# Second block of a two-block Trainium2 kernel: its input transposed without the norm's factor, which is applied behind the products

## The chip, the cores and the metric

The kernel is one program on 1 core of one Trainium2 chip. The metric is the device time of one execution in microseconds (us). Three runs of the kernel before took 1331.56, 1333.13 and 1335.11 us; the median is 1333.13 us.

Engine names: PE is TensorE's matmul, PEld its weight load, DVE VectorE, ACT ScalarE, POOL GpSimd, SP SyncE (here it issues transfers only).

## What is computed

Two blocks follow each other over 512 tokens of width 1024. The first (normalised projection, stick-breaking attention beside an RWKV-7 group, output projection, a mixture of 32 experts) ends in `rmsnorm(h, final_norm_g)`. That is the input x of the second, cut here to what the change touches:

```
h = rms_norm(x, norm_gain)                     # x * rsqrt(mean(x*x) + 1e-6) * gain
proj = h @ w_in
qa, ka, va, qb, kb, vb, ga, gb, mg = split(proj)
qa = head_rms_norm(qa, q_norm_a) * scale       # per head of 64
ka = head_rms_norm(ka, k_norm_a)
ya = banded_attention(qa, ka, va, ...) * silu(ga)
qb, kb = head_rms_norm(qb) * scale, head_rms_norm(kb)
yb = (softmax-weighted sum of three dilated groups of qb, kb, vb) * silu(gb)
gates = sigmoid(mg + b_merge)
merged = gates[0] * (ya @ w_branch_a) + gates[1] * (yb @ w_branch_b)
x = x + merged @ w_out
```

Both norms before `w_in` multiply each token by one number, so x reaches `w_in` as h * r * (final_norm_g * norm_gain), with one r per token.

## The kernel before

Tokens are four tiles of 128 (index i, NT = 4) and the width is eight blocks of 128 (index k, KD = 8). Every float32 product is made of three matmuls on rounded halves: `split` (L197) writes a high part by ACT (L206, or L203 without a scale) and a low part by DVE (L207, or L204), and `mm3` (L210) multiplies high by high (L212), high by low and low by high (L213, L214). The Tile framework's scheduler sets the order of each engine's instructions; a few calls pin it.

**End of block one.** `combine` (L1313) adds the experts' result to the residual tile `hres`: for each token tile and half of the width a group of matmuls `cb` (L1320) into PSUM, then one DVE add (L1324). In its last call it runs `last(i)` (L1345) behind each token tile. That makes both norms' sums, by an ACT square with a sum (L1354) and by a DVE multiply-and-sum (L1359; for tile 0 by POOL and ACT, L1356 and L1357), the factor r by a power on POOL (L1363), and a diagonal matrix `dg3` of it (L1364). `ahead` (L1328) has loaded and split the first section of the second block's weights.

**Start of the second block** (`phase3`). `turn(k, i0, n)` (L1478) makes block k of the transposed input: a matmul of a tile of `hres` with `dg3` (L1483) transposes it and multiplies by r at once. Two tiles share a call; `split` with the scale gg then gives `ah` and `al` (L206 and L207 on 128x256), 16 times.

**The sections.** `w_in` is 33 sections of 256 columns, each a 1 MB load (`load`, L1467) on SP's queue. A token-major section (`tok`, L1508) makes 96 matmuls `tm` in two halves of the weights; a feature-major one (`fm`, L1535) 48 matmuls `fm` over 512 tokens, in two. The first, at 0 and 256, are q of attention A, 512 is its k and v. `normed` (L1547) gives each token tile to a sink: squares on ACT (L1542), a copy to `raw` (L1543), a DVE reduction to `qss` (L1544), then `rsqrt` (DVE L282, POOL power L287, four numbers a token). `turned` (L1551) scales `raw` on DVE to `qsc` (L1555), transposes it on PE (`qT`, L1559) and copies it by ACT (L1561). `after_k` sends v through DRAM by POOL's queue (L1649, L1650). Gates (`gated`, L1864: sigmoid on ACT, two DVE multiplies, L1871 to L1873, and a split) and merge gates (`mg_sink`, L1908) are feature-major. The normalised x is written to DRAM from `hres` (DVE L1856, SP L1858).

## Time and profile before

| | |
|---|---|
| median of 3 runs | 1333.13 us |
| the profiled execution | 1333.91 us |
| its span, first to last instruction | 1331.9 us |
| PE busy | 1231.4 us, 92% of the span |
| DVE, ACT, POOL busy | 701.0, 483.3 and 231.6 us |
| mean granted TensorE clock | 0.958 of full |

The span is what the rows cover; the other 2.0 us of the execution lie around it. Times of rows count from the start of the span. A row of a timeline gives start, duration, engine, line, operation, and in brackets the idle time before it with what ended it. A busy PE is not PE at full speed: the granted clock (PEclk) has two levels, 1.00 (2.4 GHz) and 0.50 (1.2 GHz).

### The profile page before, as it was taken

What the parts mean: (1) busy time and instruction counts of PE and PEld (TensorE: products, weight loads), DVE (VectorE), ACT (ScalarE), POOL (GpSimd) and SP (SyncE); (2) the same over time, 40 slices, a digit from 0 to 9 for tenths busy, and PEclk for the clock granted to TensorE, in tenths of its full rate; (3) what the DMA queues carried; (4) which work ended last, traced back from release to release, by engine and by line L of the source; (5) the groups of instructions that cost most, each with busy time, mean ns of one, the idle gap of its engine ahead of it and who ended that gap; (6) DMA issues with size and microseconds to landing.
All of it is one profiled execution on the core that took longest, in us unless ns stands there. A gap on an engine that the chain in (4) does not pass through costs nothing.

```text
span 1331.9 us, 22066 instructions
## 1 busy us (share of the span) xinstructions
PE 1231.4 (92%) x8889; PEld 965.8 (73%) x8889; DVE 701.0 (53%) x1603; ACT 483.3 (36%) x999; POOL 231.6 (17%) x323
## 2 busy tenths in 40 slices
...
GB/s 310 77 39 57 57 41 32 33 64 52 140 102 390 257 389 422 422 422 421 424 184 69 121 78 64 88 62 99 70 92 65 82 81 64 145 93 79 80 140 67
DMA packets 45050, 198.87 MB, mean 149 GB/s; under 512 B 11639, under 2 KB 14105, under 8 KB 27792
## 3 DMA queue, kind: packets, MB, share of 16 engines
...
q14 instruction: 34, 0.28, 0.1%
...
## 4 chain that ended last, share of the span: by engine, by line
PE 50%; issue 9%; DVE 3%; ACT 3%; POOL 1%; DMA 1%; ACTq 0%; DVEq 0%; POOLq 0%
PE tm L212 7%; PE tm L213 7%; PE tm L214 7%; PE gu L1260 6%; PE fm L214 4%; PE fm L212 4%; PE fm L213 4%; PE pd L1283 3%; PE az L1601 2%; PE pbT L1818 1%; PE qT L1559 1%; ACT Pb L1612 1%; PE oa L1700 1%; PE paT L1686 1%; DMA fd<-znt 1%
## 5 line engine op out<-in xcount | busy, mean ns | idle before, releaser
L212 PE MATMUL tm<-wh,ah 128*128 128x256 f32 x800 | 231.6, 290 | 5.3 <-ACT vb L1726 5.3
L214 PE MATMUL tm<-wh,al 128*128 128x256 f32 x800 | 227.3, 284 | 0.0
L213 PE MATMUL tm<-wl,ah 128*128 128x256 f32 x800 | 227.0, 284 | 0.3 <-DVE wl L204 0.3
L204 DVE TENSOR_TENSOR wl<-w,wh 128x1024 fp32r<-128x1024 f32 (+1 forms) x124 | 144.9, 1169 | 149.1 <-ACT wh L203 148.7
L203 ACT ACTIVATE wh<-w 128x1024 fp32r<-128x1024 f32 (+1 forms) x124 | 124.1, 1002 | 260.3 <-PE tm L213 96.5
L212 PEld LDWEIGHTS tm<-wh,ah 128*128 128x128 f32 x800 | 152.2, 190 | 12.2 <-ACT vb L1726 5.5
L213 PEld LDWEIGHTS tm<-wl,ah 128*128 128x128 f32 x800 | 152.5, 191 | 0.8 <-DVE wl L204 0.6
L214 PEld LDWEIGHTS tm<-wh,al 128*128 128x128 f32 x800 | 151.8, 190 | 1.4 <-issue 1.3
L287 POOL TENSOR_TENSOR qss<-qss,nhalf 128x4 f32<-128x4 f32 x60 | 63.6, 1074 | 200.6 <-DVE qss L282 200.3
L212 PE MATMUL u<-xh,wh 128*128 128x512 f32 x176 | 75.7, 430 | 5.1 <-ACT xh L371 4.2
L212 PE MATMUL fm<-ah,wh 128*128 128x512 f32 x192 | 76.0, 396 | 0.0
L214 PE MATMUL fm<-ah,wl 128*128 128x512 f32 x192 | 75.9, 395 | 0.1
L213 PE MATMUL fm<-al,wh 128*128 128x512 f32 x192 | 75.9, 395 | 0.0
L214 PE MATMUL u<-xh,wl 128*128 128x512 f32 x176 | 73.7, 419 | 2.0 <-DVE wl L204 2.0
L213 PE MATMUL u<-xl,wh 128*128 128x512 f32 x176 | 74.3, 422 | 1.3 <-DVE xl L372 1.3
L1260 PE MATMUL gu<-eg,xgT 128*64 128x256 f32 x512 | 66.9, 396 | 2.3 <-DMA eg<-in_exp_w_gate_dram 1.9
L1283 PE MATMUL pd<-ed,hTs 128*64 128x512 f32 x256 | 64.8, 600 | 2.6 <-ACT hTs L1273 2.1
L1260 PE MATMUL gu<-eu,xgT 128*64 128x256 f32 x512 | 63.3, 380 | 0.0
L1263 ACT ACTIVATE hm<-gu 128x256 f32<-128x256 f32 x16 | 6.1, 384 | 146.1 <-PE gu L1260 101.6
L1264 DVE TENSOR_TENSOR hm<-hm,gu 128x256 f32<-128x256 f32 x16 | 6.7, 420 | 98.1 <-ACT hm L1263 98.1
L1260 PEld LDWEIGHTS gu<-eg,xgT 128*64 128x64 f32 x512 | 38.5, 142 | 26.3 <-issue 8.3
L1260 PEld LDWEIGHTS gu<-eu,xgT 128*64 128x64 f32 x512 | 39.5, 137 | 19.8 <-issue 2.3
...
## 6 DMA issues: line engine op xcount, KB each, us to landing
w<-in_w_dram SPq DMA_DIRECT2D x33, 1024.0 KB, 4.8
eg<-in_exp_w_gate_dram SPq DMA_DIRECT2D x32, 1024.0 KB, 19.7
eu<-in_exp_w_up_dram SPq DMA_DIRECT2D x32, 1024.0 KB, 19.4
ed<-in_exp_w_down_dram SPq DMA_DIRECT2D x32, 1024.0 KB, 19.7
...
yd<-hres POOLq DMA_DIRECT2D x1, 4096.0 KB, 15.9
...
yt<-yd SPq DMA_DIRECT2D x4, 1024.0 KB, 19.8
```

The costliest lines, as they stand in the source:

```text
L203: i = nc.scalar.activation(hi, src, AF.Copy)
L204: j = nc.vector.tensor_tensor(lo, src, hi.bitcast(F), op=OP.subtract)
L212: mm(out, lh, rh, start=first, stop=False)
L213: mm(out, lh, rl, start=False, stop=False)
L214: mm(out, ll, rh, start=False, stop=last)
L287: nc.gpsimd.tensor_tensor(out, out, e if len(out.shape) == 2 else e.rearrange("p (a b) -> p a b", b=out.shape[2]), op=OP.pow)
L1260: nc.tensor.matmul(ph[es, c0:c0 + 256], xt[:, c, es], EW[n, 2 * q + k][:, c, :], start=(c == 0), stop=(c == 7))
L1283: nc.tensor.matmul(pd[es, :], hT[:, c, es], EW["d", 2 * q + k][:, c, hf * 512:(hf + 1) * 512], start=(c == 0), stop=(c == 1))
L1559: nc.tensor.transpose(ps[:, i * 128:(i + 1) * 128], sc[:, i, :], eye)
L1601: nc.tensor.matmul(pz[j][:, off:off + k1 - k0], qt[rows, i * 128:(i + 1) * 128], kt[rows, k0:k1], start=True, stop=True)
L1612: nc.scalar.activation(Pt[:, n, j, 0:N], Pt[:, n, j, 0:N], AF.Exp, bias=nm[:, n, j:j + 1], scale=-1.0, accum_out=sm[:, n, j:j + 1])
L1686: nc.tensor.transpose(ps[:, m * 128:(m + 1) * 128], Pt[:, 0, h, b - k0:b - k0 + 128], eye)
```

## The change

- `combine`'s last call goes over the left halves of all four token tiles first, then over the right halves.
- `last(i)` makes only the sums, all four by DVE (POOL's share is gone), and for i = 3 the factor r of all tiles in one power of four columns, with e = 1e-6 / r², which each head's norm needs since the unscaled values go through it. `dg3` is gone.
- `turn(k)` makes four plain transposes (against the identity) into one PSUM bank and one split of 512 columns, 8 times.
- `factors()`, behind section 0: PE transposes r and e (8 rows of 128), ACT copies them, SP writes them to DRAM (`rd`), and reads them back as `rr` (a token's numbers on its partition) and `rrb` (r over all 512 tokens on every partition).
- The factor is applied where it is wanted: in the head norms (`head_factors` for sections 0 and 256, 16 columns at once; a DVE instruction with `rr` in later ones), by POOL on attention A's v, as ACT's scale in the copies of B's v, and by a DVE multiply with `rrb` (`scaled`) on each of the 24 feature-major products that are gates.

The diff, cut where lines only make way:

```diff
-        def combine(ys, after=None):
-            for i in range(NT):
-                for hf in range(2):
-                    ps = self.pa("cb") if after and i % 2 else self.p1("cb", "pw" if hf else "so")
+        def combine(ys, last=False):
+            for m in range(2 * NT):
+                    hf, i = (m // NT, m % NT) if last else (m % 2, m // 2)
+                    ps = self.pa("cb") if last and m // 2 % 2 else self.p1("cb", "pw" if m % 2 else "so")
...
-                if after:
-                    after(i)
...
         def last(i):
...
-            if i == 0:
-                nc.gpsimd.tensor_tensor(junk, h, self.fg, op=OP.mult)
-                nc.scalar.activation(junk, junk, AF.Square, accum_out=s1)
-            else:
-                nc.vector.tensor_tensor_reduce(junk, junk, self.fg2, 1.0, 0.0, op0=OP.mult, op1=OP.add, accum_out=s1)
+            nc.vector.tensor_tensor_reduce(junk, junk, self.fg2, 1.0, 0.0, op0=OP.mult, op1=OP.add, accum_out=s1)
+            if i < NT - 1:
+                return
+            s0, s1, r0, r, e = (self.st3[:, k, :] for k in range(5))
 
             ts(r, s0, 1e-6 / D, 1e-12, op0=OP.mult, op1=OP.add)
             stt(r, s1, 1.0 / D, r, op0=OP.mult, op1=OP.add)
-            nc.gpsimd.tensor_tensor(r, r, self.nhalf[:, 0:1], op=OP.pow)
-            ts(self.dg3[:, i, :], self.ident, r, None, op0=OP.mult)
+            ts(e, r, 1e-6, None, op0=OP.mult)
+            nc.gpsimd.tensor_tensor(r, r, self.nhalf[:, 0:NT], op=OP.pow)
...
-        def turn(k, i0, n):
+        def turn(k):
             ps = self.pb("x3T")
-            for j in range(n):
-                i = i0 + j
-                nc.tensor.matmul(ps[:, j * 128:(j + 1) * 128], self.h[:, i, k * 128:(k + 1) * 128], self.dg3[:, i, :],
-                                 start=True, stop=True)
...
+            for i in range(NT):
+                nc.tensor.transpose(ps[:, i * 128:(i + 1) * 128], self.h[:, i, k * 128:(k + 1) * 128], eye)
+            o = lambda z: z[:, k, :].rearrange("p (r l) -> p r l", r=4)
+            self.split(ps.rearrange("p (l r) -> p r l", r=4), o(ah), o(al), gg[:, k:k + 1])
...
+        def factors():
+            rd = self.DR.tile([2 * NT, 128], F, name="rd")
+            ps = self.p1("rT", "pw")
+            nc.tensor.transpose(ps[0:2 * NT, 0:128], self.st3[:, 3:5, :].rearrange("p a i -> p (a i)"), eye)
+            z = self.junk[0][0:2 * NT, 0, 0:128]
+            nc.scalar.activation(z, ps[0:2 * NT, 0:128], AF.Copy)
+            nc.sync.dma_start(rd, z)
+            nc.sync.dma_start(rr, bass.AP(tensor=rd.tensor, offset=rd.offset, ap=[[4, 128], [512, 2], [1, 4]]))
+            return nc.sync.dma_start(rrb, bass.AP(tensor=rd.tensor, offset=rd.offset, ap=[[0, 128], [1, 512]]))
+
+        def scaled(ps):
+
+            z = ps.rearrange("p (r l) -> p r l", r=4)
+            tt(z, z, rrb.rearrange("p (l r) -> p r l", r=4), op=OP.mult)
+            return ps
...
+        def head_factors(ss):
+
+            nc.vector.scalar_tensor_tensor(ss, ss, 1.0 / 64, rr[:, 1, :, None].to_broadcast([128, NT, 4]), op0=OP.mult, op1=OP.add)
+            nc.gpsimd.tensor_tensor(ss, ss, self.nhalf[:, 0:16].rearrange("p (i h) -> p i h", h=4), op=OP.pow)
...
         def after_k(x):
             r, s = x
+            nc.gpsimd.tensor_tensor(r[:, :, 128:256], r[:, :, 128:256], rr[:, 0, :, None].to_broadcast([128, NT, 128]), op=OP.mult)
...
+        for i in range(NT):
             next(proj)
+            self.last(i)
+        with self.tc.issue_after(factors().ins):
+            self.rsqrt(self.st3[:, 2, :], self.st3[:, 0, :], 1.0 / D, 1e-6)
+            next(proj)
...
             def f(j, ps):
                 z = new("sg", F)
+                scaled(ps)
                 nc.scalar.activation(z, ps, AF.Sigmoid)
...
-                nc.scalar.activation(mg[:, 2 * c + j, :], ps, AF.Sigmoid, bias=self.pc("b_merge_2", 2 * c + j))
+                nc.scalar.activation(mg[:, 2 * c + j, :], scaled(ps), AF.Sigmoid, bias=self.pc("b_merge_2", 2 * c + j))
```

How the change moves instructions at the places the prediction speaks of. PE, at the end of block one (`cb` is L1320, `x3T` the transposes into the second block, `tm` section 0's products), a piece of the difference, - before and + changed:

```order
 L1320 MATMUL cb<-yl,C 128x512
-L1320 MATMUL cb<-yh,C 128x512
-L1320 MATMUL cb<-yl,C 128x512
-L1483 MATMUL x3T<-dg_6023,hres 128x128 x20
+L1478 MATMUL x3T<-ident,hres 128x128 x2
+L1320 MATMUL cb<-yh,C 128x512
+L1320 MATMUL cb<-yl,C 128x512
+L1478 MATMUL x3T<-ident,hres 128x128 x6
 L212 MATMUL tm<-wh_5826,ah 128x256
 L213 MATMUL tm<-wl_5827,ah 128x256
 L212 MATMUL tm<-wh_5826,ah 128x256
 L213 MATMUL tm<-wl_5827,ah 128x256
```

The last group `cb` stands behind the first two transposes now, and the rest of the 32 transposes come in fours between products (64 in twos before). Of section 0's 96 products 64 now stand behind the last transpose, 79 before.

DVE, behind section 0 (`qss` a head's sums, `qsc` the scaled q, `wl_6410` the first half of section 512's low weights and `wl_6504` the second), in the changed kernel:

```order
L204 TENSOR_TENSOR wl_6410<-w_6407,wh_6409 128x1024
L1549 SCALAR_TENSOR_TENSOR qss<-qss,rr 128x16
L1561 TENSOR_REDUCE qss<-qsq 128x4
L1577 TENSOR_TENSOR qsc<-raw,qss 128x4x64
L1561 TENSOR_REDUCE qss<-qsq 128x4
L1577 TENSOR_TENSOR qsc<-raw,qss 128x4x64
L204 TENSOR_TENSOR wl_6504<-w_6407,wh_6503 128x1024
L1561 TENSOR_REDUCE qss<-qsq 128x4 x2
L1549 SCALAR_TENSOR_TENSOR qss<-qss,rr 128x16
L1577 TENSOR_TENSOR qsc<-raw,qss 128x4x64 x6
```

The same place before:

```order
L1544 TENSOR_REDUCE qss<-qsq 128x4
L282 TENSOR_SCALAR qss<-qss 128x4
L1555 TENSOR_TENSOR qsc<-raw,qss 128x4x64 x2
L204 TENSOR_TENSOR wl_6451<-w_6448,wh_6450 128x1024
L1544 TENSOR_REDUCE qss<-qsq 128x4
L282 TENSOR_SCALAR qss<-qss 128x4
L1544 TENSOR_REDUCE qss<-qsq 128x4
L282 TENSOR_SCALAR qss<-qss 128x4
L204 TENSOR_TENSOR wl_6545<-w_6448,wh_6544 128x1024
L1544 TENSOR_REDUCE qss<-qsq 128x4 x2
L282 TENSOR_SCALAR qss<-qss 128x4 x2
L1555 TENSOR_TENSOR qsc<-raw,qss 128x4x64 x6
```

Before, nothing there needs a transfer. Now the first L1549 needs `rr`, and the reductions of section 256, the scaled q and `wl_6504` are queued behind it.

SP's queue, in the changed kernel (`w3` are the sections' weights, 512 and 768 and the one behind, `x2d` the normalised x):

```order
L1463 DMA w3_6407<-in_w2_dram 128x2048
L1493 DMA rd_6252<-junk_5837 8x128
L1463 DMA w3_6595<-in_w2_dram 128x2048
L1494 DMA rr_6121<-rd_6252 128x2x4
L1495 DMA rrb_6122<-rd_6252 128x512
L1882 DMA x2d_5835<-hres_67 128x1024 x4
L1463 DMA w3_6776<-in_w2_dram 128x2048
```

The write stands ahead of a 1 MB load and the reads behind it; before, the four `x2d` stores stood between the load of 512 and that of 768.

## Rows read from the trace of the kernel before

**Rows 1.** the page's chain of work that ended last, shares of the span

```profile
PE 50%; issue 9%; DVE 3%; ACT 3%; POOL 1%; DMA 1%; ACTq 0%; DVEq 0%; POOLq 0%
```

**Rows 2.** stretches of the run-up to section 0: columns in the first line

```profile
core 0: us, PE busy (x) PEld busy (x) DVE busy (x) ACT busy (x) POOL busy (x), PEclk, DMA share, GB/s
...
733.00:735.00 2.00, 1.98 (x9) 2.00 (x10) 1.70 (x3) 0.47 (x1) 0.00 (x0) 0.50 0.66 262
...
738.00:739.00 1.00, 1.00 (x8) 1.00 (x8) 0.48 (x1) 0.43 (x1) 0.00 (x0) 0.74 0.00 0
```

**Rows 3.** groups of instructions, 700 to 775 us (busy us, mean ns, idle before)

```profile
L1324 DVE TENSOR_TENSOR hres<-hres,cb 128x512 f32<-128x512 f32 x15 | 9.9, 683 | 2.0 <-PE cb L1320 1.9
...
L207 DVE SCALAR_TENSOR_TENSOR yl<-pd,tb,yh 128x512 fp32r<-128x512 f32 x2 | 1.5, 746 | 0.7 <-ACT yh L206 0.7
...
L207 DVE SCALAR_TENSOR_TENSOR al<-x3T,gg,ah 128x256 fp32r<-128x256 f32 x16 | 7.5, 480 | 5.2 <-ACT ah L206 5.1
...
L206 ACT ACTIVATE ah<-x3T,gg 128x256 fp32r<-128x256 f32 x16 | 7.5, 472 | 11.9 <-PE x3T L1483 11.8
...
L1359 DVE CUSTOM_DVE_ANT_0 junk<-junk,fg 128x1024 f32<-128x1024 f32 x3 | 4.0, 1340 | 0.0
...
L204 DVE TENSOR_TENSOR wl<-w,wh 128x1024 fp32r<-128x1024 f32 x7 | 8.5, 1220 | 4.2 <-ACT wh L203 4.2
...
L1354 ACT ACTIVATE junk<-hres 128x1024 f32<-128x1024 f32 x4 | 4.2, 1054 | 5.6 <-DVE hres L1324 5.6
...
L203 ACT ACTIVATE wh<-w 128x1024 fp32r<-128x1024 f32 x6 | 6.3, 1053 | 9.4 <-PE tm L213 9.4
```

**Rows 4.** timeline, the end of block one and sections 0 to 512

```profile
710.85 1.95 DVE L1324 TENSOR_TENSOR hres<-hres,cb 128x512 f32<-128x512 f32 x3 [0.89 <-PE cb L1320]
...
720.04 0.68 DVE L1324 TENSOR_TENSOR hres<-hres,cb 128x512 f32<-128x512 f32 x1
...
741.04 0.61 PE L1483 MATMUL x3T<-dg,hres 128*128 128x128 f32 x4
...
750.99 0.39 ACT L1542 ACTIVATE qsq<-tm 128x256 f32<-128x256 f32 x1 [1.61 <-PE tm L214]
...
764.49 0.74 DVE L1544 TENSOR_REDUCE qss<-qsq 128x4 f32<-128x256 f32 x2
...
767.88 1.09 PE L1559 MATMUL qT<-ident,qsc 128*128 128x128 f32 x8
```

**Rows 5.** groups of instructions, DVE and POOL, 700 to 775 us and whole span

```profile
L1555 DVE TENSOR_TENSOR qsc<-raw,qss 128x256 f32<-128x256 f32 x8 | 3.0, 421 | 4.7 <-POOL qss L287 4.3 <-PE qT L1559 0.4
...
L461 POOL TENSOR_TENSOR rnt<-rnt,nhalf 128x16 f32<-128x16 f32 x2 | 6.7, 3368 | 10.0 <-DVE rnt L460 10.0
...
L724 POOL TENSOR_TENSOR O<-O,gs 128x512 f32<-128x512 f32 x4 | 4.2, 1042 | 0.3
```

**Rows 6.** DMA issues of the whole span: KB each, median us from issue to landing

```profile
w<-in_w_dram SPq DMA_DIRECT2D x33, 1024.0 KB, 4.8
...
sd<-zst ACTq DMA_DIRECT2D x4, 16.0 KB, 2.0
```

**Rows 7.** DMA issues from 910 to 935 us, a crowded stretch

```profile
w<-in_w_dram SPq DMA_DIRECT2D x1, 1024.0 KB, 9.8
```

**Rows 8.** timeline, attention A's k and v

```profile
779.00 0.74 POOL L1649 DMA_DIRECT2D vad<-raw  x1 [2.01 <-ACT raw L1543]
...
782.78 1.01 PE L1559 MATMUL qT<-ident,qsc 128*128 128x128 f32 x4 [2.12 <-DVE qsc L1555]
```

**Rows 9.** stretches of the same place, columns as in rows 2

```profile
782.00:784.00 2.00, 1.22 (x6) 1.25 (x7) 0.63 (x2) 0.18 (x1) 0.00 (x0) 0.72 0.96 389
...
784.00:786.00 2.00, 2.00 (x10) 1.49 (x9) 0.00 (x0) 1.98 (x2) 0.70 (x1) 0.50 0.10 41
```

**Rows 10.** stretches of the gates beside attention B, columns as in rows 2

```profile
1100.00:1110.00 10.00, 9.88 (x44) 7.82 (x43) 9.86 (x29) 5.33 (x7) 0.00 (x0) 1.00 0.33 107
...
1120.00:1130.00 10.00, 10.00 (x94) 7.90 (x95) 2.69 (x5) 1.54 (x3) 0.00 (x0) 1.00 0.29 107
```

More of the change, by code (lines that the diff above doesn't have):

```diff
@@ L1342, in ahead @@
             self.x2d = self.DR.tile([512, 1024], F, name="x2d")
-            self.st3 = self.t(self.E, "st3", [128, 4, NT])
+            self.st3 = self.t(self.E, "st3", [128, 5, NT])
+            self.junk = [e_("junk") for _ in range(2)]
         def last(i):
-            if i == 0:
-                e_ = lambda name, dt=F: self.slot([128, 2, D], dt, name, True)
-                self.junk = [e_("junk") for _ in range(2)]
-                self.dg3 = e_("dg3").rearrange("p a b -> p (a b)")[:, 0:512].rearrange("p (i q) -> p i q", i=NT)
             h, junk = self.h[:, i, :], self.junk[i // 2][:, i % 2, :]
             self.dump("h2", h, lambda d: d[i * 128:(i + 1) * 128, :])
-            s0, s1, r0, r = (self.st3[:, k, i:i + 1] for k in range(4))
+            s0, s1 = (self.st3[:, k, i:i + 1] for k in (0, 1))
             nc.scalar.activation(junk, h, AF.Square, accum_out=s0)
-            if i == 0:
-                nc.gpsimd.tensor_tensor(junk, h, self.fg, op=OP.mult)
-                nc.scalar.activation(junk, junk, AF.Square, accum_out=s1)
-            else:
-                nc.vector.tensor_tensor_reduce(junk, junk, self.fg2, 1.0, 0.0, op0=OP.mult, op1=OP.add, accum_out=s1)
+            nc.vector.tensor_tensor_reduce(junk, junk, self.fg2, 1.0, 0.0, op0=OP.mult, op1=OP.add, accum_out=s1)
+            if i < NT - 1:
+                return
+            s0, s1, r0, r, e = (self.st3[:, k, :] for k in range(5))
             ts(r, s0, 1e-6 / D, 1e-12, op0=OP.mult, op1=OP.add)
             stt(r, s1, 1.0 / D, r, op0=OP.mult, op1=OP.add)
-            nc.gpsimd.tensor_tensor(r, r, self.nhalf[:, 0:1], op=OP.pow)
-            ts(self.dg3[:, i, :], self.ident, r, None, op0=OP.mult)
+            ts(e, r, 1e-6, None, op0=OP.mult)
+            nc.gpsimd.tensor_tensor(r, r, self.nhalf[:, 0:NT], op=OP.pow)
+        self.last = last
         up, ys, rows = None, [], collect()
@@ L1385, in phase2 @@
             up = nxt
-        combine(ys, last)
+        combine(ys, True)
         self.dump("tb", tb)
@@ L1544, in sink @@
                 red(ss[:, i, :], sq.rearrange("p (h t) -> p h t", t=64), axis=AX.X, op=OP.add)
-                self.rsqrt(ss[:, i, :], ss[:, i, :], 1.0 / 64, 1e-6)
+                if c0 > 256:
+                    ts(ss[:, i, :], ss[:, i, :], 1.0 / 64, rr[:, 1, i:i + 1], op0=OP.mult, op1=OP.add)
+                    nc.gpsimd.tensor_tensor(ss[:, i, :], ss[:, i, :], self.nhalf[:, 0:4], op=OP.pow)
             yield from tm(c0, sink)
+            if c0 == 256:
+                head_factors(raws[0][1])
+                head_factors(ss)
             return raw, ss
@@ L1725, in f @@
                 def f(i, ps):
-                    nc.scalar.activation(dst[:, i, :], ps, AF.Copy)
+                    nc.scalar.activation(dst[:, i, :], ps, AF.Copy, scale=rr[:, 0, i:i + 1])
                 return f
@@ L1758, in att_b @@
                         yield
-                z = q_("zst", [128, NT, 8], bufs=2)
+                z = q_("zst", [128, NT, 8])
                 for g in (1, 2):
```

19 lines of the change are left out of this document (7 added, 12 removed).

## The prediction, made before the changed kernel ran

> **What bounds the kernel now.** I read the chain of waits on the page first: half the span is PE and 9% is issue on it [rows 1]. So the place to look at is where PE waits or runs at the low clock, and the change touches such a place: the passage from block one's last sums to section 0. In the stretches of the run-up [rows 2] the reader is to see that PE is full from 733 us on (1.98 of 2.00 us) and yet at a clock of 0.50, and that the clock is 0.74 in the slice from 738 to 739, so it rises near 738.4: some 5.3 us of dense work at the low level. Behind it the timeline [rows 4] has the last transposes at 741.04 to 741.65 and section 0's last pair of tiles at ACT at 750.99. In between stand 79 products (counted in the trace and in the order): (750.99 - 741.65) / 79 = 0.118 us each, at full clock. At the low clock PE started ten in 2.00 us [rows 9], 0.20 us each. I call E0 the end of section 0 on PE; before it is 751.0.
>
> What holds PE back ahead of 733 is a chain over four engines per token tile: add, square and multiply-and-sum, power, diagonal, transposes, split. Its last add ran from 720.04 to 720.72 [rows 4], and 16 splits of 0.48 us on DVE follow transposes that wait for the diagonals [rows 3].
>
> **1. The passage, a gain of 13.7.** Without `dg3` the transposes need only the adds. These stand back to back on DVE now: the first ran at 710.85, eight at 0.683 are 5.5, so 716.3, and I allow 0.5 of handovers from PE: 716.8 [rows 3, 4]. Then DVE has eight low splits of 512 columns, which no row shows with these strides: between 0.746 (the split of `yl`, 512 columns) and 0.96 (two of 0.48); I take 0.8, nearer the first since it is one instruction. With four multiply-and-sums of 1.34 and 1.1 of small ones that is 6.4 + 5.4 + 1.1 = 12.9, so the last split ends at 716.8 + 12.9 = 729.7 [rows 3]. ACT has less: four squares of 1.05, eight high splits of at most 2 x 0.472 and two `wh` of 1.05 are 13.9, from about 714.2 (its first square needs only the first tiles), 728.1; it is hidden behind DVE [rows 3]. The last transposes stand ahead of a high and a low split: 729.7 - 0.8 - 0.85 - 0.5 = 727.5 (handovers estimated). By the order, 64 products are left then. If PE, dense from there, stays low as long as it did before, 5.3 us, it does 26 at 0.20 and 38 at 0.118: E0 = 727.5 + 5.3 + 4.5 = 737.3, and the gain is 13.7. Bounds: all 64 at full clock, 735.1 (15.9); all at the low one, 740.3 (10.7).
>
> **2. The round trip, a cost of 3.9.** This is the wait that the change adds. The first L1549 on DVE needs `rr`, behind it in DVE's queue stand the reductions and `qsc` of section 256 and the second half of section 512's low weights, and `qT` on PE waits for `qsc`. PE has cover: before, `qT` ran at 767.88 [rows 4], E0 + 16.9, with no idle time, and its place behind section 0 is the same in the order. When does `rr` come? PE transposes r and ACT copies, then SP writes at about E0 + 1.6. A small write landed after 2.0 [rows 6], so SP could read at E0 + 3.7; but a 1 MB load stands between them on SP's queue. Bounds: `rr` unaffected by it, E0 + 3.7 + 2.0 = 5.7; or all of a load in a crowded stretch, 9.8 [rows 7], and then its own, E0 + 15.5. I take the median load, 4.8 [rows 6], and 1.0 more for the small read itself, half of the 2.0 since part of it can run beside the load: E0 + 9.5. It is nearer the lower end, as one crowded load stands against 33 behind the median.
> From `rr` to `qT`: L1549 0.2, power of 16 columns 3.37, two reductions at 0.37 each and two `qsc` at 0.42 between, a low weight split 1.22, two reductions 0.74, L1549 0.2, a second power 3.37, the last `qsc` 0.42 [rows 3 to 5]: 11.1, with handovers 11.3. Thus `qT` at E0 + 20.8, 3.9 later than the 16.9. Below, it can't be less than 1.6: section 256's last reduction ended at 765.23, E0 + 14.2, and behind it stand 0.2 + 3.37 + 0.42 and handovers, 18.5. Above, with `rr` at 15.5, it is 9.9.
> Here a rule differs from what I took. By the Trainium skill, DMA: Bandwidth & Descriptors, section Anatomy of one DMA, a transfer has a fixed part of about 2.0 us, which for 4 KB is nearly all of it, and the row of small writes agrees with its 2.0; by that rule alone `rr` would be there at E0 + 5.7. By the same page, section Queues, rings and completion order, each engine takes descriptors in ring order, so a 1 MB load issued ahead would come first, which gives the sum's case or D; no row of before shows a small read right behind such a load.
>
> **3. The clock after that idle, a cost of 1.6.** PE already has such a gap: after 2.12 us idle it began `qT` at 782.78 [rows 8], and the clock was 0.72 and then 0.50 in the two stretches from 782 [rows 9]. That loses 2 x 0.28 + 2 x 0.50 = 1.6. An idle time of 3.9 I price the same. Bounds: 0 if PE's gap closes, 2.7 (half of the 5.3 us of part 1) if the low level lasts as long as there.
>
> **4. Attention A's v, a cost of 0.8.** POOL multiplies v by r ahead of the store and of the power that K's `qT` waits for. A POOL instruction on 128x512 takes 1.04 [rows 5], the store was issued at 779.00, and PE idled 2.12 there [rows 8], so nothing hides it but the two products that now stand ahead of this `qT` (0.24). Bounds: 0 and 1.3.
>
> **5. The feature-major multiplies, a cost of 1.5.** Of 24 on DVE the 16 of the merge gates lie in stretches like that from 1120 to 1130, where DVE is busy 2.69 of 10 us [rows 10]: hidden, at most 1 us each beside a PE that is busy 10.00 there; without that cover they would be 15. Of the eight gates three stand in the stretch from 1100, where DVE has 9.86 of 10 us [rows 10]. Each costs 0.68 (an add of 512 columns out of PSUM) to 0.96 (two strided halves) [rows 3]. They cost 0 if PE isn't held by DVE (it was busy 9.88 there too) and 2.9 if it is: I take the middle, 1.5. B's v costs nothing: the copies only get another scale.
>
> **Sum:** -13.7 + 3.9 + 1.6 + 0.8 + 1.5 = -5.9. Against the profiled execution (1333.91, which is 0.8 above the median) 1328.0; against the median of 1333.13, **1327.2 us**.
>
> **Rivals.**
> *B, the round trip is mostly hidden.* `rr` lands without regard to the load, as the small writes did [rows 6]; term 2 falls to 1.6. Sum -13.7 + 1.6 + 1.6 + 0.8 + 1.5 = -8.2: 1324.9, and 1323.4 if the gates cost nothing. For it: only 4 KB move. Against it: the load is ahead in the queue. 0.22.
> *C, the low clock lasts.* Before, the dense stretch was products for the most part [rows 2]; now transposes come in fours between 32 products, with waits for the splits. If PE gets its full clock only after section 0, the gain is 10.7: sum -2.9, 1330.2. Against it: 64 of section 0's 96 products stand behind the last transpose, nothing between them. By the Trainium skill, TensorE: Matmul & The Clock Gate, section Part 4: PE-mode transpose, a transpose doesn't engage the full clock, as it doesn't count as busy in the same way. That would speak against this change, as it puts transposes where a multiplication by the diagonal stood; the trace of before, at 0.50 among both, can't part the two. 0.16.
> *D, slower: `rr` comes late.* At E0 + 15.5, `qT` comes 9.9 later and PE idles as long, with the clock loss at 2.7: sum -13.7 + 9.9 + 2.7 + 0.8 + 1.5 = +1.2: 1334.3. It decides from about E0 + 14.3 on; slower by over 0.3% (4 us, about what a measurement of this kernel tells from no change) needs E0 + 18.3. For it: the broadcast, the x2d stores and the bias tables move in the same microseconds, and one load of 1 MB took 9.8 [rows 7]. Against it: the median is 4.8. 0.13.
> That the change isn't what it says can be left out: the order shows transposes against the identity and no diagonal.
>
> **How the numbers follow.** My forecast has 0.45, B 0.22, C 0.16, D 0.13, and 0.04 stays for what I can't name, half of it slower. Faster by over 0.3% is below 1329.1: seven in ten of the forecast (0.32), B (0.22) and a quarter of C (0.04), 0.58. Slower is above 1337.1: the upper half of D (0.07) and 0.03: 0.10. The rest, 0.32, lies within. The range goes from B with hidden gates and the best of term 1, 1323.4 - 2.2 = 1321.2, taken as 1320.5, to D with the gates' upper price and its `rr` a little later: 1336.0.
>
> **What would show it.** Right: in the stretches, PE dense from about 727.5 and section 0's last squares at ACT near 737; then a wait of DVE at L1549 for the transfer, an idle time of PE of 2 to 5 us ahead of the first `qT`, and `qT` near 758; the landing of `rr` 5 to 7 us behind its issue. B: that landing near 2 us and the idle time under 2. C: a clock of 0.50 until the end of section 0. D: the landing beyond 10 us. The gates: DVE full and PE waiting for `sg` in the attention-B stretch. I am wrong altogether if DVE's last split ends past 735, if PE's order behind section 512 gives new waits in attention B, or if the time saved ahead of 760 is given back at a transfer that doesn't come earlier.

## The result and the profile after

| | before | changed |
|---|---|---|
| median of 20 runs | 1333.70 us | 1326.01 us |
| lowest to highest | 1330.62 to 1338.73 | 1321.69 to 1332.04 |
| the profiled span | 1331.9 us | 1323.8 us |
| mean granted clock | 0.958 | 0.965 |

The ratio is 0.9941, with a 95% interval of 0.9928 to 0.9954: 7.7 us faster between the medians, where 5.9 were forecast. The page of the changed kernel, its busy times and its chain (columns as in [rows 1] for the second line):

```profile
PE 1221.9 (92%) x8858; PEld 954.9 (72%) x8858; DVE 723.7 (55%) x1605; ACT 484.8 (37%) x990; POOL 227.1 (17%) x315
...
PE 52%; DVE 5%; DMA 4%; ACT 3%; issue 1%; POOL 1%; ACTq 0%; DVEq 0%; POOLq 0%
```

PE's busy time fell from 1231.4 to 1221.9 us; where, stands below under the passage. DVE's rose from 701.0 to 723.7, mainly by the 24 multiplies by `rrb` (1.08 each).

The runs spread by more than any single term, and most of the spread lies in block one, which the change hardly touches: one fixed product of PE near its end (the 507th `gu` with `eg`) began between 689.5 and 697.5 us in the fourteen profiles of this case. So I compare by stages: the time between the starts of the same PE instructions, counted in each trace. The stages are block one; then to the last L214 product of section 0; to the first `qT`; to the 120th `az` (through attention A); to the 620th L214 product; to the 34th `fm` of L213 (the gates beside attention B); to the end.

| run | block one | section 0 | first qT | attention A | to 620th | gates | rest |
|---|---|---|---|---|---|---|---|
| before | 691.5 | 59.20 | 17.20 | 145.51 | 149.60 | 64.52 | 204.4 |
| changed | 690.1 | 41.17 | 23.75 | 145.73 | 150.41 | 68.10 | 204.6 |
| e1_no_rr_wait | 690.6 | 41.17 | 18.42 | 146.88 | 150.87 | 67.89 | 204.6 |
| e2_rr_pool_queue | 695.9 | 41.18 | 19.81 | 145.86 | 150.67 | 67.42 | 204.7 |
| e3_gates_16_columns | 690.4 | 41.17 | 23.66 | 145.70 | 150.60 | 65.95 | 204.7 |
| e4_tile_order | 693.2 | 41.41 | 21.89 | 144.74 | 150.45 | 67.96 | 204.5 |
| e5_idle_before_split | 689.7 | 41.80 | 22.58 | 147.41 | 150.14 | 67.47 | 205.2 |
| e5b_idle_before_split | 689.5 | 44.45 | 18.37 | 147.40 | 149.77 | 68.03 | 204.5 |
| e6_gate_on_pool | 697.5 | 41.16 | 23.33 | 145.77 | 150.58 | 70.17 | 204.5 |
| e7_factors_on_pe | 694.4 | 41.18 | 19.44 | 148.27 | 150.95 | 67.56 | 202.3 |
| e7b_..._same_layout | 696.5 | 41.15 | 19.32 | 147.65 | 149.80 | 67.66 | 204.8 |
| e8_pad_16_bytes | 694.9 | 41.16 | 23.83 | 146.52 | 151.43 | 67.42 | 202.1 |
| e9_rrb_in_order | 694.2 | 41.17 | 19.40 | 147.47 | 149.67 | 66.71 | 204.5 |
| e10_all_three | 693.1 | 41.17 | 18.39 | 144.23 | 150.42 | 66.72 | 204.5 |

The changed kernel against before: -1.4 in block one (its spread), **-18.0** to the end of section 0, **+6.6** to the first `qT`, +0.2, +0.8, **+3.6** in the gates, +0.2. The sum is -8.0; the two spans differ by 8.1.

**The passage.** Stretches of the changed kernel, columns as in [rows 2]:

```profile
715.00:720.00 5.00, 3.66 (x26) 2.97 (x26) 4.87 (x12) 5.00 (x9) 0.00 (x0) 1.00 0.02 3
...
720.00:725.00 5.00, 5.00 (x43) 4.87 (x44) 4.86 (x9) 4.04 (x8) 0.00 (x0) 1.00 0.00 0
...
745.00:750.00 5.00, 0.96 (x9) 0.76 (x7) 2.11 (x6) 1.32 (x4) 2.92 (x1) 1.00 0.96 394
...
750.00:755.00 5.00, 4.54 (x25) 4.33 (x25) 1.95 (x6) 0.56 (x1) 2.90 (x1) 0.66 0.59 213
```

PE is at 1.00 from 715 on and full from 720, where before it was full only from 733 and then at 0.50 [rows 2]. The timeline's last adds, last four transposes and section 0's last pair of tiles:

```profile
712.56 2.63 DVE L1324 TENSOR_TENSOR hres<-hres,cb 128x512 f32<-128x512 f32 x4 [0.17 <-PE cb L1320]
...
723.36 0.60 PE L1478 MATMUL x3T<-ident,hres 128*128 128x128 f32 x4
...
731.54 0.38 ACT L1559 ACTIVATE qsq<-tm 128x256 f32<-128x256 f32 x1 [1.61 <-PE tm L214]
```

The adds end at 715.2 (720.72 before, [rows 4]), the last transposes at 724.0 (741.65), and section 0 at 731.5 (750.99). The splits and sums in between, groups of 700 to 740 us:

```profile
L1350 DVE CUSTOM_DVE_ANT_0 junk<-junk,fg 128x1024 f32<-128x1024 f32 x4 | 4.8, 1216 | 0.0
...
L207 DVE SCALAR_TENSOR_TENSOR al<-x3T,gg,ah 128x512 fp32r<-128x512 f32 x8 | 5.7, 746 | 0.3
...
L206 ACT ACTIVATE ah<-x3T,gg 128x512 fp32r<-128x512 f32 x8 | 5.2, 689 | 1.3 <-PE x3T L1478 1.0 <-issue 0.3
```

Eight splits of 0.746 stand in place of sixteen of 0.480 [rows 3], and DVE is never idle for long (0.3 us before them).

What PE gained in this stage can be read from the stage as one stretch, before and changed, and from the stretch before in which the clock was low:

```profile
691.47:750.67 59.20, 47.65 (x256) 36.27 (x253) 38.26 (x75) 20.84 (x39) 11.31 (x10) 0.80 0.27 98
...
718.00:738.50 20.50, 14.16 (x57) 12.71 (x58) 14.21 (x35) 8.51 (x17) 4.49 (x4) 0.50 0.28 104
```
```profile
690.06:731.23 41.17, 37.00 (x225) 26.52 (x221) 31.84 (x55) 17.03 (x29) 6.55 (x5) 0.96 0.18 65
```

Idle time fell from 11.55 to 4.17 us: 7.4. Of the 14.16 us of work at 0.50 half would go at full clock: 7.1, an estimate. And work went as well: a product with the diagonal is two PE instructions for each of the 32 tiles, a plain transpose one.

```profile
L1483 PE MATMUL x3T<-dg,hres x64: 270/421/583, 718.2 to 741.4; 128*128 128x128 f32 x64
```
```profile
L1478 PE MATMUL x3T<-ident,hres x32: 270/272/329, 713.6 to 723.7; 128*128 128x128 f32 x32
```

At the 0.11 us from start to start that both take at full clock, 32 fewer are 3.5 us. The three make the 18.0.

**The round trip.** The issues on SP's queue, the first instruction on DVE that needs `rr`, the `qsc` behind it that waits for POOL's power, an ACT square that waits for DVE's reduction behind that, PE's next product, and the first `qT`:

```profile
735.32 0.35 SPq L1463 DMA_DIRECT2D w<-in_w_dram  x1
...
736.35 0.38 SPq L1494 DMA_DIRECT2D rr<-rd  x1
...
736.78 0.79 SPq L1495 DMA_DIRECT2D rrb<-rd  x1
...
745.18 0.18 DVE L1549 SCALAR_TENSOR_TENSOR qss<-qss,rr 128x16 f32<-128x16 f32 x1 [5.60 <-DMA rr<-rd]
...
748.39 0.43 DVE L1577 TENSOR_TENSOR qsc<-raw,qss 128x256 f32<-128x256 f32 x1 [2.71 <-POOL qss L1550]
...
749.18 0.38 ACT L1559 ACTIVATE qsq<-tm 128x256 f32<-128x256 f32 x1 [2.75 <-DVE qss L1561]
...
749.90 0.39 PE L212 MATMUL tm<-wh,ah 128*128 128x256 f32 x1 [4.04 <-ACT raw L1560]
...
754.98 1.09 PE L1581 MATMUL qT<-ident,qsc 128*128 128x128 f32 x8 [0.46 <-DVE qsc L1577]
```

`rr` was issued at 736.35, one microsecond behind the 1 MB load, and DVE went on at 745.18: 8.8 us. In the stretches above, PE is idle for 4.0 us of 745 to 750, and then the clock is 0.66 on the mean of 750 to 755.

**Attention A's v and the gates.** POOL's multiply and K's `qT` (2.93 idle, against 2.12 in [rows 8]):

```profile
765.52 1.04 POOL L1670 TENSOR_TENSOR raw<-raw,rr 128x512 f32<-128x512 f32 x1 [1.78 <-ACT raw L1560]
...
770.58 0.64 PE L1581 MATMUL qT<-ident,qsc 128*128 128x128 f32 x4 [2.93 <-DVE qsc L1577]
```

The multiply by `rrb`, the copies of v, and PE's waits from 1030 to 1117 us (us in total, times, longest):

```profile
L1500 DVE TENSOR_TENSOR fm<-fm,rrb x24: 1070/1084/1101, 1082.5 to 1230.5; 128x512 f32<-128x512 f32 x24
...
L1749 ACT ACTIVATE vb<-tm,rr x16: 453/462/475, 920.8 to 1077.8; 128x256 f32<-128x256 f32 x16
```
```profile
PE fm L212 <- ACT vb L1749: 1.1, 1, 1.1
...
PE fm L214 <- DVE wl L204: 0.7, 1, 0.7
```

Before, the same copies took 0.37 us in the median, and PE had neither of these waits:

```profile
L1726 ACT ACTIVATE vb<-tm x16: 360/372/386, 935.6 to 1087.5; 128x256 f32<-128x256 f32 x16
```

### The profile page after: what moved, and what is told of

Read it like the earlier page. It is cut to its first block, busy times and chain, and to the rows that moved or that the text cites. A ratio compares the mean times of both kernels' runs of the same rounds, so it can differ in the third digit from the quotient of the medians.

```text
span 1323.8 us, 21996 instructions
## 1 busy us (share of the span) xinstructions
PE 1221.9 (92%) x8858; PEld 954.9 (72%) x8858; DVE 723.7 (55%) x1605; ACT 484.8 (37%) x990; POOL 227.1 (17%) x315
## 4 chain that ended last, share of the span: by engine, by line
PE 52%; DVE 5%; DMA 4%; ACT 3%; issue 1%; POOL 1%; ACTq 0%; DVEq 0%; POOLq 0%
PE gu L1260 8%; PE tm L212 6%; PE tm L213 6%; PE tm L214 6%; PE pd L1283 4%; PE fm L214 4%; PE fm L213 4%; PE fm L212 4%; PE cb L1320 3%; DMA eg<-in_exp_w_gate_dram 2%; PE az L1623 1%; PE pbT L1841 1%; PE qT L1581 1%; ACT Pb L1634 1%; PE paT L1709 1%
## 5 line engine op out<-in xcount | busy, mean ns | idle before, releaser
L214 PE MATMUL tm<-wh,al 128*128 128x256 f32 x800 | 227.4, 284 | 0.0
L213 PE MATMUL tm<-wl,ah 128*128 128x256 f32 x800 | 227.0, 284 | 0.3 <-DVE wl L204 0.3
L213 PEld LDWEIGHTS tm<-wl,ah 128*128 128x128 f32 x800 | 152.6, 191 | 1.4 <-issue 0.8
L214 PEld LDWEIGHTS tm<-wh,al 128*128 128x128 f32 x800 | 152.4, 191 | 1.1 <-issue 0.8
L1564 POOL TENSOR_TENSOR qss<-qss,nhalf 128x4 f32<-128x4 f32 x52 | 55.3, 1078 | 172.0 <-DVE qss L1563 172.0
L214 PE MATMUL fm<-ah,wl 128*128 128x512 f32 x192 | 76.1, 396 | 0.7 <-DVE wl L204 0.7
L213 PE MATMUL fm<-al,wh 128*128 128x512 f32 x192 | 75.9, 395 | 0.0
L214 PE MATMUL u<-xh,wl 128*128 128x512 f32 x176 | 73.5, 418 | 2.1 <-DVE wl L204 2.1
L213 PE MATMUL u<-xl,wh 128*128 128x512 f32 x176 | 74.0, 421 | 1.5 <-DVE xl L372 1.5
L1500 DVE TENSOR_TENSOR fm<-fm,rrb 128x512 f32<-128x512 f32 x24 | 26.0, 1084 | 57.2 <-PE fm L214 57.1
```

The costliest lines, as they stand in the source:

```text
L213: mm(out, lh, rl, start=False, stop=False)
L214: mm(out, ll, rh, start=False, stop=last)
L1500: tt(z, z, rrb.rearrange("p (l r) -> p r l", r=4), op=OP.mult)
L1564: nc.gpsimd.tensor_tensor(ss[:, i, :], ss[:, i, :], self.nhalf[:, 0:4], op=OP.pow)
```

## The experiments

All are edits of the changed kernel. Of the stages, only the one that an edit aims at is read.

**e1_no_rr_wait.** No wait for the transfer.

```diff
-            nc.vector.scalar_tensor_tensor(ss, ss, 1.0 / 64, rr[:, 1, :, None].to_broadcast([128, NT, 4]), op0=OP.mult, op1=OP.add)
+            ts(ss, ss, 1.0 / 64, 1e-6, op0=OP.mult, op1=OP.add)
```

> The changed kernel, with the constant 1e-6 in place of 1e-6/r^2 in the head norms of sections 0 and 256 (this leaves a part of the norm's constant out), so that the first work behind section 0 waits for no transfer. Theory W (the wait for rr costs most of what was lost between section 0 and attention A): the first qT comes about 18 us behind the end of section 0 in place of 23.4, PE's idle time of 4.0 us ahead of it is gone, and the run is 4 to 6 us faster than the changed kernel. Rival (the time is taken back later, by a transfer that isn't earlier): the first qT as early, but the end at most 2 us earlier.

1321.76 us, ratio to before 0.9895 (0.9864 to 0.9926). The first `qT` comes 18.42 behind section 0 (23.75), and of PE's idle time ahead of it 0.95 is left:

```profile
750.17 1.09 PE L1581 MATMUL qT<-ident,qsc 128*128 128x128 f32 x8 [0.95 <-DVE qsc L1577]
```

So the wait for `rr` and what follows it cost 5.3 us, and theory W holds at this place. 1.2 us came back in attention A (146.88 against 145.73), where the clock was 0.50 for 6.8 us from 764.9 on, in place of 3.4; e7b below tells more.

**e2_rr_pool_queue.** The read of `rr` on POOL's queue.

```diff
-            nc.sync.dma_start(rr, bass.AP(
+            nc.gpsimd.dma_start(rr, bass.AP(
```

> The changed kernel with the read of rr issued on POOL's queue, where no 1 MB load stands ahead of it; the load, the x2d stores and rrb stay where they are. Theory Q (the queue: rr waits behind the load that is ahead of it on SP's queue): rr is there 2 to 4 us after its issue in place of 8.8, and the run is 3 to 5 us faster. Rival X (crowding: the DMA engines are full with the load, the stores and rrb, whatever the queue): rr takes 6 to 9 us, and the run is within 2 us of the changed kernel.

1326.52 us, ratio 0.9927 (0.9898 to 0.9955), not to be told from the changed kernel by its runs. The first `qT` came after 19.81, 3.9 earlier. `rr` took 4.7 us from issue to landing:

```profile
rr<-rd POOLq DMA_DIRECT2D x1, 4.0 KB, 4.7
```

That is between the two theories: without a load ahead on its queue the read is faster, but not at the 2.0 of a small write [rows 6]. The order on DVE moved too (a weight split behind the wait, 1.5 us of PE), so this run alone decides nothing. Four other runs set the two apart, below at e5b.

**e4_tile_order.** The sums in the old order.

```diff
-                    hf, i = (m // NT, m % NT) if last else (m % 2, m // 2)
+                    hf, i = m % 2, m // 2
```

> The changed kernel with block one's last sums in the old order (token tile outside, half inside). Theory G (the gain comes from the diagonal being gone: PE has no idle time of 2.5 us at 716 and keeps the full clock): section 0 ends at most 1.5 us later than in the changed kernel, the clock stays at 1.00. Rival O (the order of the halves is what keeps PE fed): the clock falls to 0.50 behind the last sums and section 0 ends 4 us later or more.

1326.70 us, ratio 0.9944 (0.9922 to 0.9967). Section 0's stage is 41.41 against 41.17: the order of the halves is worth 0.2 us. By elimination the gain lies with the diagonal and what went with it (the doubled PE instructions, the 16 splits, POOL's share of the sums), which no run takes one by one. Where PE waits for the later adds the clock stays at 1.00 (columns as in [rows 2]):

```profile
718.00:720.00 2.00, 0.95 (x6) 0.54 (x4) 2.00 (x7) 2.00 (x5) 0.00 (x0) 1.00 0.00 0
```

**e5_idle_before_split.** Two multiplies on DVE ahead of the splits.

```diff
+        for _ in range(2):
+            self.tc.keep_in_program_order(tt(self.junk[1][:, 1, :], self.h[:, 3, :], self.fg, op=OP.mult))
```

> The changed kernel with two DVE multiplies of 1024 columns (1.28 us each, results unused) between the last adds and the first split, so that PE runs out of work for about 2.5 us there. Theory C (the gain beyond my sum is the clock, which falls after such an idle time): the clock is 0.50 in stretches between 718 and 728 and section 0 ends 4 to 8 us later, clearly more than the 2.5 added. Rival (only the work counts): section 0 ends 1 to 2.5 us later at a clock of 1.00.

A failed experiment: the scheduler put the multiplies behind the splits, PE didn't run out of work, and section 0 ended 0.6 later. But by its order on SP `rr` went out ahead of the 1 MB load, and still it took 5.8 us:

```profile
737.16 0.39 SPq L1496 DMA_DIRECT2D rr<-rd  x1
...
743.00 0.18 DVE L1551 SCALAR_TENSOR_TENSOR qss<-qss,rr 128x16 f32<-128x16 f32 x1 [5.76 <-DMA rr<-rd]
```

**e5b_idle_before_split.** The same with the scale of the splits behind the multiplies.

```diff
-        nc.gpsimd.tensor_tensor(gg, self.par[:, r0:r0 + KD], self.par[:, r1:r1 + KD], op=OP.mult)
+        zz = self.junk[1][:, 1, :]
+        tt(zz, self.h[:, 3, :], self.fg, op=OP.mult)
+        tt(zz, zz, self.fg, op=OP.mult)
+        tt(gg, self.par[:, r0:r0 + KD], self.par[:, r1:r1 + KD], op=OP.mult)
+        nc.vector.scalar_tensor_tensor(gg, zz[:, 0:KD], 0.0, gg, op0=OP.mult, op1=OP.add)
```

> The changed kernel with the scale gg made behind two DVE multiplies of 1024 columns (1.28 us each) that wait for the last add, so that the first split really waits and PE runs out of work for 2.5 us or more near 716. Theory C (the gain beyond my sum is the clock, which falls after such an idle time): the clock is 0.50 in stretches between 718 and 728 and section 0 ends 5 to 9 us later than in the changed kernel, clearly more than the time added. Rival (only the work counts): section 0 ends 2 to 4 us later, at a clock of 1.00.

PE idled from 712.94 to 718.32, and the clock did fall:

```profile
716.00:718.00 2.00, 0.00 (x0) 0.00 (x0) 2.00 (x5) 0.56 (x2) 0.00 (x0) 0.96 0.00 0
...
718.00:720.00 2.00, 1.68 (x7) 1.57 (x8) 2.00 (x5) 1.89 (x4) 0.00 (x0) 0.50 0.00 0
...
720.00:722.00 2.00, 2.00 (x13) 1.86 (x11) 1.87 (x4) 1.32 (x2) 0.00 (x0) 0.69 0.00 0
...
722.00:724.00 2.00, 2.00 (x17) 1.92 (x17) 2.00 (x4) 0.74 (x2) 0.00 (x0) 1.00 0.00 0
```

By these shares it was low for about 3.4 us, from 717.8 to 721.3, and section 0 ended only 3.3 us later: theory C, as I had put it (5 to 9 us), falls, and so does the rival's clock of 1.00. This one idle time didn't make the 20 us at 0.50 of the kernel before. There PE stopped again and again (2.6 us at 715.6, 0.7, 3.2, 0.5, 0.2 and 1.5 at 731.5), by these rows of before for a diagonal or a split:

```profile
718.18 1.22 PE L1483 MATMUL x3T<-dg,hres 128*128 128x128 f32 x4 [2.56 <-DVE dg L1364]
...
724.53 2.08 PE L1483 MATMUL x3T<-dg,hres 128*128 128x128 f32 x8 [3.19 <-DVE al L207]
```

That these stops kept the clock low there is a reading; no run repeats them.

This run also has the shortest read: `rr` was issued at 738.88 with no load ahead, into DMA engines that were nearly idle, and DVE went on 1.8 us later:

```profile
738.88 0.39 SPq L1498 DMA_DIRECT2D rr<-rd  x1
...
740.66 0.17 DVE L1553 SCALAR_TENSOR_TENSOR qss<-qss,rr 128x16 f32<-128x16 f32 x1 [5.01 <-DMA rr<-rd]
```

Stretches of e5b from 738 and of the changed kernel from 736, where `rr` was issued; the last two columns are the DMA engines' busy share and GB/s:

```profile
738.00:740.00 2.00, 2.00 (x20) 2.00 (x19) 0.00 (x0) 0.07 (x1) 0.00 (x0) 1.00 0.11 29
```
```profile
736.00:738.00 2.00, 2.00 (x19) 2.00 (x18) 0.00 (x0) 0.74 (x1) 0.00 (x0) 1.00 1.02 230
```

So it is crowding first: 1.8 us at a share of 0.11, against 3.4 (e4, where the load had been issued 6.3 us ahead), 5.8 (e5, no load ahead) and 8.8 (changed, the load 1.0 us ahead) at shares near 1. The crowd is the bias tables on POOL's queue (five ahead of `rr` in the changed kernel, three in e5), which were there before too but which nobody waited for, and the load; the queue adds to it, by how much these runs don't tell.

**e3_gates_16_columns.** The multiply of the eight gates on a sliver.

```diff
-                scaled(ps)
+                tt(ps[:, 0:16], ps[:, 0:16], rrb[:, 0:16], op=OP.mult)
```

> The changed kernel with the DVE multiply of the eight silu gates on 16 of their 512 columns (the rest of the gates' columns go without the factor). From the 620th L214 product of the token-major sections to the 34th of the feature-major ones PE took 64.5 us before and takes 68.1 in the changed kernel. Theory D (DVE: three or four more multiplies in a stretch where it is full): this stretch goes back to 64.5 to 66 us. Rival V (the copies of v, which ACT makes with a scale now, 0.45 in place of 0.38 us, or the new order on PE): it stays above 67 us.

The gates' stage is 65.95: of the 3.6 us lost there 2.15 are the multiplies on a full DVE. The other 1.4 stay, and with them PE's wait of 1.1 us for the copies of v; 65.95 lies at the upper edge of theory D's range, and both theories have a part. Whether the longer copies or the new order on PE make that wait, no run tells.

**e6_gate_on_pool.** The gate's last multiply on POOL.

```diff
-                tt(z.rearrange("p (r l) -> p r l", r=4), z.rearrange("p (r l) -> p r l", r=4),
+                nc.gpsimd.tensor_tensor(z.rearrange("p (r l) -> p r l", r=4), z.rearrange("p (r l) -> p r l", r=4),
```

> The changed kernel with the last multiply of a gate, which reads and writes SBUF only, on POOL in place of DVE. Theory D (DVE): DVE gets back about as much as the new multiply costs (1.07 against 1.08 us a gate), so the stretch from the 620th L214 product to the 34th feature-major one falls from 68.1 to 64.5 to 66.5 us. Rival (the chain of a gate's own steps, not DVE's load, is what PE waits for): a POOL step of about 1.04 us and two more handovers leave it at 67.5 or more.

1327.34 us, ratio 0.9951 (0.9927 to 0.9976); the gates' stage went up to 70.17. POOL needs 1.54 us for what DVE did in 1.07, and PE's waits grew to 2.2 and 1.2:

```profile
L1898 POOL TENSOR_TENSOR sg<-sg,hres x8: 1522/1542/1667, 1093.3 to 1153.4; 128x512 f32<-128x512 f32 x8
```
```profile
PE fm L214 <- DVE wl L204: 2.2, 1, 2.2
...
PE pbT L1841 <- DVE PT L1843: 1.2, 1, 1.2
```

The number is the rival's (67.5 or more), but its reason, the gate's chain, isn't shown, since a third cause shows that neither theory named. While a POOL multiply ran from 1100.73 to 1102.30, three DVE multiplies beside it took 2.11 us (0.80 in the changed kernel), one of them 1.62, and DVE came that much later to `wl`, which stands behind them and which PE waited for:

```profile
1100.58 2.11 DVE L1830 TENSOR_SCALAR Pb<-Pb,fst 128x256 f32<-128x256 f32 x3
...
1102.61 1.21 DVE L204 TENSOR_TENSOR wl<-w,wh 128x1024 fp32r<-128x1024 f32 x1
```

That is 1.3 of the 1.5 us by which this wait grew. Two more such instructions ran 1.57 and 1.23 us in place of 0.28 beside the next two.

**e7_factors_on_pe.** `rr` without DRAM.

```diff
+            for i in range(NT):
+                nc.tensor.matmul(pq[:, 8 * i:8 * i + 8], sel[:, i, :], self.st3[:, 3:5, :].rearrange("p a i -> p (a i)"), start=True, stop=True)
+            w = self.junk[1][:, 0, 0:32].rearrange("p (m j) -> p m j", j=NT)
+            tt(w, pq[:, 0:32].rearrange("p (m j) -> p m j", j=NT), msk[:, None, :].to_broadcast([128, 8, NT]), op=OP.mult)
+            red(rr.rearrange("p a i -> p i a"), w.rearrange("p (i a) j -> p i a j", a=2), axis=AX.X, op=OP.add)
-            nc.sync.dma_start(rr, bass.AP(tensor=rd.tensor, offset=rd.offset, ap=[[4, 128], [512, 2], [1, 4]]))
```

(`sel` holds shifted columns of the identity, `msk` which quarter a partition belongs to.)

> The changed kernel with rr made on the chip: four products of 8 columns on PE with a constant selection matrix, a DVE multiply with a mask and a reduction, in place of the read from DRAM; only rrb still goes through DRAM. Theory W (the wait for the transfer): the first qT comes 18.3 to 19 us behind the end of section 0 (23.75 in the changed kernel), and the run is 4 to 6 us faster than the changed one. Rival (PE's few products with a wait for POOL's power, or the transfers that remain, cost about as much): 21 us or more, and less than 2 us gained.

1325.43 us, ratio 0.9934 (0.9912 to 0.9957). The first `qT` came after 19.44, 0.4 above theory W's range and far from the rival's 21, but attention A took 2.5 us longer, and the run gained little. The median distance of the token-major products was 120 ns in place of 117 (in the last sections the mean was 120.0 against 118.3), that of the feature-major ones 227 in place of 233.

**e7b_factors_on_pe_same_layout** and **e8_pad_16_bytes** tell whether the pace is a matter of place.

```diff
-        msk = t("msk", [128, NT])
+        msk = self.selb[:, 1, 0:NT]
```

> As the run with the factors made on PE, but its mask of 4 columns lies in a buffer that is there anyway, so that the tiles behind it keep the places in SBUF that they have in the changed kernel. Theory P (that run's first qT came 4.3 us earlier and the gain was lost again because its tiles lie 16 bytes further on, with which PE's products took a median of 120 in place of 117 ns): products 117 ns, first qT 19.4 us behind the end of section 0, and a run 4 to 5 us faster than the changed kernel, about 1321 to 1322. Rival (the gain is lost to the new order of work behind section 0): products 117 ns, but at most 2 us gained.

```diff
+        msk = t("msk", [128, NT])
+        nc.gpsimd.memset(msk, 0.0)
```

> The changed kernel with an unused tile of 16 bytes a partition ahead of rr and one POOL memset of it; the order of the work on PE, DVE, ACT and SP is unchanged. Theory P (place in SBUF): the token-major products take a median of 120 ns in place of 117 and the feature-major ones 227 in place of 234, as in the run with the factors on PE. Rival (the pace is a matter of the chip or of the run): 117 and 234 ns.

The pad alone gives 120 and 227 ns, and e7b has 117 and 233 again (the 234 expected is 233 by the starts): it is the place of the tiles in SBUF. But e7b is no faster for it: ratio 0.9931 (0.991 to 0.9951), 1327.91 us. Its first `qT` is 4.4 us earlier and attention A 1.9 longer, so 2.5 remain at this place; the runs don't show them, and their interval is too wide to exclude them. In the stretches (columns as in [rows 2]) the clock is at 0.50 for longer behind K's idle time of 2.95 us:

```profile
775.00:780.00 5.00, 5.00 (x24) 4.38 (x21) 2.36 (x7) 2.85 (x7) 0.00 (x0) 0.50 0.20 54
...
780.00:785.00 5.00, 5.00 (x38) 4.53 (x37) 2.79 (x12) 1.87 (x7) 1.13 (x2) 0.90 0.00 0
```

In the changed kernel it was 0.50 for 3.4 us at 750.6 and for 3.4 at 771.1; in e7b for 6.8 at 774.1 and at none before. So the loss of clock that the first wait had caused came at the next wait here; neither theory had it. It doesn't have to come: in e4, which had no low clock at the first wait either, the same `qT` follows an idle time as long, and the clock stays at 1.00.

```profile
772.11 0.63 PE L1581 MATMUL qT<-ident,qsc 128*128 128x128 f32 x4 [2.95 <-DVE qsc L1577]
```
```profile
770.00:775.00 5.00, 2.46 (x18) 1.96 (x19) 1.04 (x3) 2.21 (x2) 1.98 (x3) 1.00 0.48 164
```

With the clock up e4's attention A takes 144.74, though no edit aims at it.

**e9_rrb_in_order.** `rrb` in the products' order, on top of e7b.

```diff
-            z = ps.rearrange("p (r l) -> p r l", r=4)
-            tt(z, z, rrb.rearrange("p (l r) -> p r l", r=4), op=OP.mult)
+            tt(ps, ps, rrb, op=OP.mult)
...
+            nc.scalar.activation(z, ps[0:NT, 0:128].rearrange("p (l r) -> p r l", r=4), AF.Copy)
+            nc.sync.dma_start(rd.rearrange("r i l -> i r l"), z)
```

> The run with the factors on PE in the same layout, and rrb stored in the order of the products' columns, so that the DVE multiply of a gate reads without strides. Theory D (DVE's load and the gate's own chain): the multiply takes about 0.70 us in place of 1.08, and the stretch from the 620th L214 product to the 34th feature-major one falls from 68.1 to 66.5 to 67.3 us. Rival (only the number of steps counts): the stretch stays at 67.8 or more.

0.70 us in place of 1.08, and the gates' stage is 66.71 against 67.66, as theory D has it:

```profile
L1510 DVE TENSOR_TENSOR fm<-fm,rrb x24: 690/699/700, 1082.7 to 1229.9; 128x512 f32<-128x512 f32 x24
```

**e10_all_three.** On top of e9, section 256's power by tile, and section 512 scaled by ACT.

```diff
+                sc = rr[:, 0, i:i + 1] if c0 == 512 else 1.0
+                nc.scalar.activation(sq, ps, AF.Square, scale=sc)
+                nc.scalar.activation(raw[:, i, :], ps, AF.Copy, scale=sc)
...
-            nc.gpsimd.tensor_tensor(r[:, :, 128:256], r[:, :, 128:256], rr[:, 0, :, None].to_broadcast([128, NT, 128]), op=OP.mult)
```

> A version meant to beat both: the factors on PE, rrb in the products' order, section 256's power by token tile as in the later sections, and section 512 (k and v of attention A) scaled by ACT in its square and its copy, so that POOL's multiply of v is gone. From the runs so far: 5 us for the wait, 0.8 for POOL's multiply, 1 to 1.5 for the gates: 1318 to 1320 us. Rival (what is taken from one wait turns up in the next): 1322 or more.

**1320.34 us** (1318.94 to 1323.82 in 5 runs), ratio to before 0.9887 (0.9868 to 0.9907), below the changed kernel's 0.9941 (0.9928 to 0.9954). It beats both, 0.3 us above the range that I expected. In its profile K's idle time is 2.29 (2.93), and behind it the clock stays at 1.00, so attention A takes 144.23. That the shorter idle time keeps the clock up isn't shown, since e4 kept it behind 2.95:

```profile
765.00:770.00 5.00, 2.27 (x19) 1.74 (x17) 0.76 (x2) 1.65 (x2) 1.96 (x3) 1.00 0.66 246
...
770.00:775.00 5.00, 5.00 (x41) 4.36 (x38) 2.85 (x10) 3.90 (x11) 0.57 (x1) 1.00 0.21 54
```

## Why the prediction was right, point by point

The direction, the place and the two costs were as forecast, and 1326.0 lies 1.2 below the 1327.2 forecast. But the terms were off, the gain and the costs both too small; that the sum comes so near is luck.

**1, the passage: 13.7 forecast, 18.0 measured, outside its bounds (10.7 to 15.9).** The step that failed is the pair "the last split ends at 729.7" and "PE stays low as long as it did before, 5.3 us". In time from the same point of block one (the changed trace is 1.4 earlier there), the last transposes ended at 725.4, not 727.5: a multiply-and-sum holds DVE for 1.14 to the next start (its mean is 1.22 in the rows above and was 1.34 in [rows 3], where the tail beside the next one counts), and a split for 0.67, not 0.8. Four and eight of them make 1.8 of these 2.1 us. And there was no low clock, 2.1 more (26 products at 0.118 in place of 0.20). Rival C, the low clock that lasts, is refuted. Its rule in the Trainium skill (TensorE: Matmul & The Clock Gate, section Part 4: PE-mode transpose), by which a transpose doesn't bring the full clock, doesn't show here: the clock was at 1.00 from 713.0, ahead of the first of the 32 transposes, which stand in fours between products, and stayed there throughout. A stretch of transposes alone was not tried. The halved PE instructions of the transposes, 3.5 us of PE's time, stand in no term: the sum goes by DVE's path up to the last transposes.

**2 and 3, the round trip and the clock: 5.5 forecast, 6.6 measured.** `rr` came at 13.7 behind section 0's end, where I took 9.5 and had 15.5 as the upper bound. So the number is nearer rival D than the forecast, though below D's point of 14.3. Term 2 priced the load ahead on the queue; first comes the crowd of DMA engines full with the bias tables, which D names. From `rr` to `qT` it took 9.8, not 11.3 (POOL's power of 16 columns ran 2.9, not 3.37), which took back a part. The rule of a fixed 2 us (Trainium skill, DMA: Bandwidth & Descriptors, section Anatomy of one DMA) is given there for transfers issued from GpSimd, while `rr` is issued on SP; it fits the one run where the engines were free, with 1.8, and rival B needed just that. The place was off by one step too: PE stopped ahead of section 512's products, not at `qT`. With DVE waiting for `rr` and then, at `qsc`, 2.7 us for POOL's power, its reductions were late, so ACT's squares (two buffers) and copies were, and PE had no free PSUM. 4.0 of the 4.5 us idle stood there. The lower bound of 18.5 for the first `qT` held to 0.1 (18.42 in e1). The clock's loss, 3.4 us at 0.50, is 1.7 against 1.6.

**4, attention A's v: 0.8 forecast, 0.8 measured** as idle time (2.93 against 2.12); of the whole stage up to the 120th `az` 0.2 is left.

**5, the gates: 1.5 forecast, 3.6 measured, above its bound of 2.9.** Two things: a multiply takes 1.08 with its strides, not at most 0.96, and "B's v costs nothing" was wrong. A scale from SBUF makes ACT's copy 0.46 in place of 0.37 us, and PE waited 1.1 us for one of them (that the longer copy makes this wait isn't shown apart from the new order). The 16 merge gates were hidden, as forecast: the rest of the kernel took 0.2 us more.

The errors nearly cancel: 4.3 more gain, against 1.1 and 2.1 more cost and some 0.4 in stages that no term named, give -6.6 in the stages for -5.9.
